# A11 B11 by quarter products, passing weight sets by VectorE or from DRAM, and an order taken from a table

## The chip, the cores and the metric

One core of a Trainium2 chip. TensorE multiplies, VectorE (DVE in the profile) and ScalarE (ACT) work on results and inputs, GpSimd (POOL) can help with sums, SyncE (SP) issues nearly all DMAs. The metric is the device time of one launch in microseconds (us).

## The reference

```python
def reference(x, w):          # x: 8 x 2048 x 2048, w: 2048 x 2048, float32
    cs = np.cumsum(x, axis=1)
    diff = cs - np.concatenate([zeros, cs[:, :-1, :]], axis=1)
    return np.matmul(diff, w)
```

The difference of a running sum is x itself, so what must be computed is x (16384 x 2048, in 128 tiles of 128 rows) times w (2048 x 2048).

## The kernel before

**Outer products.** Tiles 0 to 3 are multiplied plainly in bf16 while w arrives; this also finds w's largest element. From tile 4 on everything is float16, each row of x divided by its scale and w by its largest element. Four tiles make a group: g, h = g + 2, and g + 1, h + 1. A group is called here by the number of its first tile: 4, 8, 12, ... 124, 31 groups. Tile g is the upper half and g + 1 the lower half of a 2 x 2 block matrix, K and N are halved too, and the Strassen-Winograd scheme makes the product with seven products instead of eight: A11 B11, A12 B21, S1 T1, S2 T2, S3 T3, S4 B22 and A22 T4. S1 to S4 are sums of halves of x, made by VectorE in place (`total`); T1 to T4 are sums of weight blocks, made once. h and h + 1 do the same with the same weights. An outer product of one tile is 16 matmuls of 128 x 128 by 128 x 512, so 32 for the pair g, h.

**Inner products by quarters.** Some of the seven are taken once more by the same scheme: g is now the upper, h the lower half, and K and N are halved again. Seven quarter products of 4 matmuls, 28 instead of 32, take its place. Each needs its own weight set of four 128 x 512 blocks: t11, t12, t21, t22 as they stand, Q1 to Q4 as sums (class `Inner`). Group 4 (`group_plain`) has no inner products, groups 8 and 12 have three (A12 B21, S4 B22, A22 T4), and from group 16 on S1 T1 is the fourth (`five` in the code).

**Where results go.** A quarter product ends in one bank of PSUM (eight banks of 128 x 512 float32). An output tile `c` gets its first product by ScalarE (`keep`, L545: bank times the row's unit into SBUF) and each further one by VectorE (`add`, L548: bank times unit plus c). A quarter product that belongs to several outputs is added to each of them.

**Weight sets that pass.** [...] The fourth sets of in_2, in_4 and in_5 go through one small tile, `flow`: in a group VectorE makes one for in_2 (`less`, L501) and one for in_3 (L818), GpSimd makes those of in_5 and in_4 (`pass_fourth`, L505). In groups 8 and 12 some are written to DRAM (`spill`) and fetched back.

**Inputs.** Each tile of x is loaded in two halves (L100), weighed by ScalarE (`weigh`, L112: the sum of absolute values), scaled and narrowed to float16 (`narrow`, L143) and turned by two DMA transposes (`turn`, L156). Five half tiles of float32 (`F`) hold what is on its way: three first halves and two second halves in rotation.

**Order.** Every instruction goes through `after(engine, ...)`, which keeps each engine's instructions in the order in which the code asks for them; each engine takes its queue strictly in order. The order is written out by hand in `group`: products, adds and the steps of S2 T2 and S3 T3 (`go`, 4 matmuls each) are interleaved. Waits on data are put in by the framework.

## Time and profile before

| | us |
|---|---|
| median of 3 runs | 1502.97 (1502.04 to 1503.34) |
| the profiled execution | 1502.15 |
| its span, first to last instruction | 1500.3 |
| PE busy | 1477.7 (98%), 6793 matmuls recorded of 6799 |
| DVE busy | 1329.1 (89%) |
| ACT busy | 914.2 (61%) |
| POOL busy | 329.0 (22%) |
| HBM read, written | 151.52 MB, 136.31 MB |

The busy times come from part 1 of the page. The granted clock of TensorE is full in all slices, and the DMA engines are busy for 80 to 90% of most slices. A line of the groups reads: line of the kernel, engine, operation, tile written <- tiles read, shape, count | busy us, mean ns of one | idle us ahead of it and what ended that idle time.

### The profile page before, as it was taken

The numbers are of one execution on the slowest core, as the hardware profiler recorded it, in microseconds if no ns is written. First come the engines' busy times: TensorE is split into PE (matmuls) and PEld (weight loads), VectorE is DVE, ScalarE is ACT, GpSimd is POOL, SyncE is SP. The second block draws the span as 40 slices with busy tenths as digits, with TensorE's granted clock in tenths as the row PEclk, the third lists the DMA queues.
The fourth block names the chain that finished last, engine by engine and source line by source line (L and its number), as shares of the span: only waits on it lengthen the run. The fifth ranks groups of instructions, "written<-read, shape, count | busy, mean of one in ns | idle before, by whom it ended". The sixth has DMA issues, their size and how long they took to land.

```text
span 1500.3 us, 21209 instructions
## 1 busy us (share of the span) xinstructions
PE 1477.7 (98%) x6793; PEld 660.9 (44%) x6799; DVE 1329.1 (89%) x2419; ACT 914.2 (61%) x1301; POOL 329.0 (22%) x360
## 2 busy tenths in 40 slices
PE   8999999999999999999999999999999999999998
PEld 3444444444444444444444444444444444444443
DVE  7987778889989889998899998889998899898897
ACT  5876565665666655666656666656656656656552
POOL 0100002212221222221222221122222122222122
PEclk9999999999999999999999999999999999999999
DMA  9999989888878898878988887988888988888962
GB/s 358 358 242 273 245 229 238 238 253 237 212 231 218 243 253 224 224 229 220 250 246 213 232 226 227 256 242 214 230 214 240 252 234 220 229 220 241 254 174 106
DMA packets 378913, 354.28 MB, mean 236 GB/s; under 512 B 274929, under 2 KB 275441, under 8 KB 378673
## 3 DMA queue, kind: packets, MB, share of 16 engines
q1 hardware_dynamic: 378240, 351.09, 84.4%
q0 software_dynamic: 560, 1.84, 0.3%
q8 instruction: 53, 0.87, 0.2%
q14 instruction: 60, 0.48, 0.1%
HBM read 151.52 MB, written 136.31 MB: 192 GB/s over the span
## 4 chain that ended last, share of the span: by engine, by line
PE 74%; DVE 13%; issue 4%; DMA 4%; ACT 3%; SPq 0%; DVEq 0%; ACTq 0%
PE b L537 37%; PE b L518 35%; DVE c L548 9%; DVE inner L508 3%; PE b L250 2%; DMA W<-in_w_dram 2%; ACT c L545 2%; DMA F<-in_x_dram 1%; DVE W L501 1%; DMA x<-F 1%; DVE x L508 0%; DMA W<-in_x_dram 0%; DMA out_dram<-c 0%; ACT waste L112 0%; DVE m L129 0%
## 5 line engine op out<-in xcount | busy, mean ns | idle before, releaser
L548 DVE SCALAR_TENSOR_TENSOR c<-b,u,c 128x512 f32<-128x512 f32 x1044 | 734.1, 746 | 125.9 <-PE b L537 76.2
L518 PE MATMUL b<-W,x 128*128 128x512 f16 x3072 | 716.1, 379 | 1.5 <-ACT c L545 0.8
L545 ACT ACTIVATE c<-b,u 128x512 f32<-128x512 f32 x492 | 313.0, 680 | 274.7 <-issue 146.7
L518 PEld LDWEIGHTS <-x 128*128 128x128 f16 x3072 | 300.4, 98 | 364.7 <-DVE x L508 1.7
L143 ACT ACTIVATE F<-F,s 128x1024 f16<-128x1024 f32 x246 | 282.9, 1150 | 162.7 <-DVE s L131 158.7
L537 PE MATMUL b<-W,inner 128*128 128x512 f16 x1392 | 338.3, 379 | 0.0
L112 ACT ACTIVATE waste<-F 128x1024 uint8<-128x1024 f32 x246 | 259.8, 1056 | 119.4 <-DMA F<-in_x_dram 115.4
L537 PEld LDWEIGHTS <-inner 128*128 128x128 f16 x1744 | 168.4, 98 | 215.5 <-DVE c L548 15.4
L132 POOL TENSOR_SCALAR u<-m,uw 128x1 f32<-128x1 f32 x124 | 66.2, 539 | 809.9 <-DVE m L129 802.2
L537 PEld LDWEIGHTS <-x 128*128 128x128 f16 x1560 | 152.1, 98 | 196.0 <-issue 14.4
L537 PE MATMUL b<-W,x 128*128 128x512 f16 x968 | 234.2, 379 | 1.5
L505 POOL TENSOR_TENSOR flow<-W 128x512 f16<-128x512 f16 x140 | 163.6, 1195 | 291.1 <-PE b L537 291.1
L508 DVE TENSOR_TENSOR x<-x,x 128x1024 f16<-128x1024 f16 (+1 forms) x214 | 146.8, 698 | 6.2 <-PE b L518 1.1
L505 POOL TENSOR_TENSOR flow<-W,W 128x512 f16<-128x512 f16 x84 | 94.9, 1160 | 0.0
L537 PE MATMUL b<-flow,x 128*128 128x512 f16 x352 | 90.3, 379 | 2.6 <-DVE c L548 2.6
L508 DVE TENSOR_TENSOR inner<-x,x 128x1024 f16<-128x1024 f16 (+1 forms) x122 | 67.6, 554 | 3.3 <-DMA x<-F 3.3
L537 PE MATMUL b<-inner,x 128*128 128x512 f16 x240 | 61.6, 379 | 0.7 <-DVE x L508 0.7
L250 PE MATMUL b<-wb,xP 128*128 128x512 bf16 x234 | 56.8, 392 | 5.4 <-ACT wb L234 3.8
L537 PE MATMUL b<-inner 128*128 128x512 f16 x240 | 61.6, 379 | 0.5 <-DVE c L548 0.5
L508 DVE TENSOR_TENSOR inner<-x,inner 128x512 f16<-128x512 f16 x60 | 51.7, 862 | 0.0
L112 ACT ACTIVATION_READ_ACCUMULATOR waste<-F 128x1 f32 x246 | 46.7, 190 | 0.0
L508 DVE TENSOR_TENSOR x<-inner,x 128x1024 f16<-128x1024 f16 x62 | 42.4, 683 | 3.2
(58 smaller groups left out, 515.9 us busy)
## 6 DMA issues: line engine op xcount, KB each, us to landing
F<-in_x_dram SPq DMA_DIRECT2D x246, 512.0 KB, 5.0
out_dram<-c SPq DMA_DIRECT2D x492, 256.0 KB, 3.3
W<-in_w_dram SPq DMA_DIRECT2D x32, 512.0 KB, 9.8
W<-in_x_dram SPq DMA_DIRECT2D x16, 256.0 KB, 7.2
x<-F SPq DMA_TRANSPOSE x246, 3.3
spill<-flow SPq DMA_DIRECT2D x3, 512.0 KB, 2.7
out_dram<-o POOLq DMA_DIRECT2D x5, 256.0 KB, 3.9
out_dram<-o SPq DMA_DIRECT2D x5, 256.0 KB, 3.7
```

The source lines that it names most:

```text
L112: lambda: nc.scalar.activation(waste, where[t][i], ABS, scale=1.0 / ROW, accum_out=sums_of[t][:, i : i + 1],),
L132: after("pool", lambda: nc.gpsimd.tensor_scalar(u, m, uw, None, MUL))
L143: lambda: nc.scalar.activation(narrowed(t)[:, ds(i * NH, NH)], where[t][i], COPY, scale=s),
L250: lambda: nc.tensor.matmul(ps[r][n], xP[:, r, ko, :], wb[h, ko][:, ds(n * NB, NB)], start=(ko == 0), stop=(ko == KO - 1),),
L501: after("dve", lambda: nc.vector.tensor_tensor(dst[k], p[k], q[k], SUB))
L505: after("pool", lambda: nc.gpsimd.tensor_tensor(passed[k], i.t21[k], i.Q2[k], SUB))
L508: after("dve", lambda: nc.vector.tensor_tensor(dst.all, p.all, q.all, op))
L518: said = nc.tensor.matmul(to[n], a[k], b[k][:, n, :], start=(first and k == 0), stop=(k == KH - 1), skip_group_check=True,)
L537: said = nc.tensor.matmul(to, a[k], b[k], start=(first and k == 0), stop=(k == 3), skip_group_check=True)
L545: after("act", lambda: nc.scalar.activation(c, p, COPY, scale=u))
L548: after("dve", lambda: nc.vector.scalar_tensor_tensor(c, p, u, c, MUL, ADD))
```

## The change

**A fifth inner product.** A11 B11 is taken by quarters as well (in_1). Group 4 is as before without any, group 8 has two (A12 B21 and S4 B22), and from group 12 on (`more`) there are five: P1 = A11 B11, P2 = A12 B21, P3 = S4 B22, P4 = A22 T4, P5 = S1 T1.

**Sums in the banks.** A new class, `Quarters`, holds one inner product in four banks: h[0], h[1], g[0], g[1]. ScalarE copies product 0 from h[0] to g[0] (`first`), so that product 3 is added to it there by TensorE; products 2, 4 and 6 are added to h[0], and ScalarE copies the state after 2 and after 4 out to a tile in SBUF (`out2`, `out4`). VectorE adds these to h[1], once into g[1] (`middle`) and once in place (`last`). The four banks then hold finished sums, and each output takes one `keep` or one `add` from each. Two tiles (`rooms`) hold s1, s3 and s2, s4 in turn.

**Passing sets.** Seven weight sets pass through `flow` in a steady group. VectorE makes four of them, each in one sum of 128 x 2048 (in3.Q1, in3.Q3, in4.Q1, in1.Q1); three are fetched from DRAM (in1.Q4, in5.t21, in4.Q3), where groups 8 and 12 leave them. GpSimd makes none. All of w stands in one tile, so that one instruction can reach four blocks.

**Buffers.** `F` has four half tiles instead of five, handed out in the order in which they come free. An output tile is 128 x 1024, so it is written by one DMA of 512 KB where there were two of 256 KB.

**Order.** An operation is no longer issued where the code asks for it: `record` notes it under a label, and `emit` issues all of them sorted by a place that a table gives to each label, with a distance of 833 between groups. There are four tables: group 4, group 8, group 12, and one for all later groups.

The diff, cut to this:

```diff
+    def emit(places=None):
+        def when(op):
+            at, label = op[:2]
+            own = places[min(at, 3)]
+            return at * PERIOD + own.get(label, 0)
+
+        for _, _, engine, ask in sorted(ops, key=when) if places else ops:
+            after(engine, ask)
...
-    F = const.tile([P, 5, NH], f32, name="F")
+    F = const.tile([P, 4, NH], f32, name="F")
...
-    def pass_fourth(i):
-        for k in range(4):
-            after("pool", lambda: nc.gpsimd.tensor_tensor(passed[k], i.t21[k], i.Q2[k], SUB))
...
+        def give(self, name):
+            p, q, op = {"Q1": ("t22", "Q2", SUB), "Q4": ("t21", "Q2", SUB), "Q3": ("Q2", "t11", SUB)}[name]
...
+                tensor(f"{self.name}.{name}", flow, self.wide[p], self.wide[q], op)
+            self.b[name] = passed
...
+        def bring(self, name):
+            kept = self.kept
+            record(f"{self.name}.{name}", "sp", lambda: nc.sync.dma_start(flow, kept))
...
+        def middle(self):
+            tensor(f"{self.name}.middle", self.g[1], self.h[1], self.lent, ADD)
+
+        def last(self):
+            tensor(f"{self.name}.last", self.h[1], self.h[1], self.lent, ADD)
+
+        def slot(self, i):
+            h, g, b = self.h, self.g, self.right.b
+            to, left, right, start = (
+                (h[0], "a11", "t11", True),
+                (h[1], "s1", "Q1", True),
+                (h[0], "s2", "Q2", False),
+                (g[0], "a12", "t21", False),
+                (h[0], "s3", "Q3", False),
+                (g[1], "s4", "t22", False),
+                (h[0], "a22", "Q4", False),
+            )[i]
+            quarter(f"{self.name}.{i}", to, getattr(self, left), b[right], start)
+            if i == 0:
+                copy(f"{self.name}.first", g[0], h[0])
+            elif i in (2, 4):
+                copy(f"{self.name}.out{i}", self.lent, h[0])
...
+        P1.slot(0)
+        P1.slot(1)
+        if more:
+            in_1.bring("Q4")
+        ready["tail"]()
+        P1.three()
+        weigh(next_g, [0])
+        P2.slot(0)
+        P2.slot(1)
...
+        P3.middle()
+        P3.slot(3)
+        add("C12g+P3.g", C12g, P3.g, ug, [0])
...
+        if more:
+            in_4.bring("Q3")
```

A stretch of the last table, from P5 into P3 and on to P4, in which a smaller number goes first (`kept` gives the keeps of C22 and C12; `loadN`, `turnN` and `weighN` are those of the tile N places behind the group's first):

```diff
+            'P5.2': 219, 'P5.1': 221, 'P5.out2': 222, 'weigh6.0': 223, 'P5.3': 260,
+            'keep C22g.0': 261, 'keep C12g.0': 262, 'P5.s4': 264, 'P5.s3': 265, 'P5.4': 268,
+            'P5.middle': 320, 'P5.out4': 328, 'P5.5': 329, 'keep C22g.1': 330, 'keep C12g.1': 341,
+            'weigh6.1': 342, ... 'P5.6': 406, 'keep C22h.0': 409, 'P3.0': 414, 'keep C12h.0': 415,
+            'P3.first': 417, 'P3.1': 427, 'narrow6.0': 429, 'narrow6.1': 430, 'P3.2': 434,
+            'P3.out2': 449, 'P3.4': 450, 'keep C22h.1': 451, 'keep C12h.1': 452, 'P3.middle': 469,
+            'P3.out4': 472, ... 'P3.5': 485, 'in4.Q1': 487, 'turn4.1': 489, 'turn6.0': 490,
+            'put0.1': 493, 'P4.0': 497, 'P3.6': 498, 'turn6.1': 505, 'P4.1': 507, 'in4.Q3': 509,
+            'load7.0': 511, ... 'P4.4': 689, 'in1.Q1': 690,
```

## The prediction

> **What bounds the kernel now.** I read the page first, then the chain of waits, then one group cut out of the middle, engine by engine. A group that takes four of the seven outer products by quarters (28 of the 31 do) shows its period in the list of the chain's longest pieces:

> ```profile
> 451.66 6.91 PE b L518 x32
> 497.04 6.91 PE b L518 x32
> ```

> The two starts are 45.38 us apart, and 6.91/32 = 0.2159 us is one matmul of 512 columns. The group has 4 x 28 + 3 x 32 = 208 of them, 44.91 us, so TensorE stands still for 0.47 us in a group. The windows view of just this stretch says how full the others are:

> ```profile
> 820.03:865.41 45.38, 45.26 (x210) 20.25 (x209) 40.97 (x76) 27.87 (x40) 11.18 (x12) 1.00 0.86 235
> ```

> The columns are the length, then PE, PEld, DVE, ACT and POOL busy, the granted clock (1.00), the DMA share and GB/s. TensorE is the bound, VectorE is 90% busy, ScalarE 61%. Where the 0.47 us goes shows in the chain of the same group and in two engines' timelines:

> ```profile
> 842.78 1.36 DVE inner L508
> ...
> 848.52 0.75 DVE c L548
> 849.27 0.04 issue
> 849.32 1.90 PE b L537 x8
> ```
> ```profile
> 841.46 1.40 DVE L508 TENSOR_TENSOR x<-x,x 128x512 f16<-128x512 f16 x1
> 842.77 1.37 DVE L508 TENSOR_TENSOR inner<-x,inner 128x512 f16<-128x512 f16 x1
> ...
> 844.38 12.31 DVE L548 SCALAR_TENSOR_TENSOR c<-b,u,c 128x512 f32<-128x512 f32 x18
> ...
> 864.35 0.42 DVE L508 TENSOR_TENSOR inner<-x,inner 128x512 f16<-128x512 f16 x1
> ```
> ```profile
> 839.18 4.68 POOL L505 TENSOR_TENSOR flow<-W 128x512 f16<-128x512 f16 x4 [4.42 <-PE b L537]
> ```

> While GpSimd makes a passing weight set (839.18 to 843.86), two VectorE sums that take 0.42 us elsewhere take 1.40 and 1.37. The 18 scaled adds behind them run without a gap, and a product that needs their bank starts 0.25 us late. A second stop, 0.21 us at 858.85, is an add between two products of one bank.

> **The change, part by part.** *Fewer matmuls.* A11 B11 by quarters is 28 matmuls for 32. The 28 groups fall from 208 to 204; group 12 has all five sets, so from 212 to 204; group 8 has two, so from 212 to 216. That is 28 x 4 + 8 - 4 = 116 matmuls x 0.2159 = 25.0 us on the path. The floor of a group becomes 204 x 0.2159 = 44.04 us.

> *VectorE, per group, from the table's labels.* Before: 35 adds. After: 20 adds at 12.31/18 = 0.68, 13.7; 10 sums that read a bank and an SBUF tile and write a bank (`middle`, `last`); 20 half-width sums at 0.38 (0.42 alone, 0.34 in a run), 7.6; 8 outer sums at 0.65, 5.2; 4 passing sets of 128x2048; 4 mean-and-reciprocal pairs at 0.37, 1.5. No row shows a sum that writes a bank. Bounds are 0.42 (both inputs SBUF, f16) and 0.75 (the add, which reads a bank); it is nearest the add, so 0.70, 7.0 in all, or 4.2 to 7.5. [...] A 128x2048 sum is 1.22 by the line through 0.42 (512 elements) and 0.69 (1024); four of the narrow ones took 1.42 (row L818, `flow`), so 1.1 to 1.5; 4.9. Sum 39.9 of 44.04: fuller in share than now, but not the bound.

> *ScalarE.* The weighing, narrowing and 16 keeps stay at 27.9. Added are 15 copies from a bank, ten to SBUF and five into another bank:

> ```profile
> L545 ACT ACTIVATE c<-b,u 128x512 f32<-128x512 f32 x492 | 313.0, 680 | 274.7 <-issue 146.7 <-PE b L537 102.0 <-PE b L518 18.6
> L270 ACT COPY o<-b 128x512 f32<-128x512 f32 x9 | 4.7, 601 | 0.0
> ```

> By the copy row 0.52 to 0.60 each, by the keep 0.64 to 0.68: 7.8 to 10.2, I take 0.60, 9.0. ScalarE comes to 36.9, 84% of the group. No row has it write a bank; I take the same price, the bounds hold it.

> *The new links.* Now VectorE adds each quarter product where it lies; after, the products of a set lean on one another through copies. Each of five sets has: product 0, copy, product 2, copy, `middle`, product 5; product 4, copy, `last`, product 6. These ride on TensorE's queue: what waits there holds all products behind it. So I laid the steady table out by hand: 51 steps of four matmuls, 0.864 each, from P1's first at 0, and a result usable 0.2 us after its step (last matmul 379 ns against 216, plus the 0.04 of the chain). The tightest stretch is from P5 to P3. P5.2 ends at 18.1; ScalarE then runs without a pause through out2, a weighing, two keeps, out4, two keeps, a weighing, two keeps, P3's first copy, two narrowings, out2 and the keeps of C22h and C12h, to 30.2. P3.middle writes the bank that these two read, so it runs 30.2 to 30.9, and P3.5 is due at 31.1: 0.15 us to spare. Elsewhere it is 0.35 (P4.0 behind an add), 0.45 (P5.4 behind s3, which waits until P5.1 has read s1), 0.5 (P5.6 behind out4) and more. Nothing is late if durations hold. Some will not quite: I take 0.3 us lost in a group, between 0 and the 0.47 of now.

> *GpSimd.* Its 8 sums a group go: about 1.9 us of VectorE time and the 0.25 us stop with them. What is left there is four one-column products. The passing sets now come through one `flow` tile seven times in a group: four by VectorE (the shortest opening 3.4 us for 1.2 of work), three from DRAM.

> *DMA and SyncE.* Three fetches of 512 KB are added, 1.57 MB on 10.5. 16 writes of 256 KB become 8 of 512. SP has 8 issues fewer there and 3 more, at 0.35 to 0.5 each: a gain hidden anyway. Its queue is in order, and a fetch waits for a product to have read `flow`, with loads and turns behind it. The openings are 7.8, 7.8 and 6.05 us (in4.Q3, after P4.1 and before P4.4). The nearest rows for the landing:

> ```profile
> F<-in_x_dram SPq DMA_DIRECT2D x246, 512.0 KB, 5.0
> ...
> spill<-flow SPq DMA_DIRECT2D x3, 512.0 KB, 2.7
> ...
> flow<-spill SPq DMA_DIRECT2D x1, 512.0 KB, 5.0
> ```

> 5.0 plus 0.4 to issue fits all three, with 0.65 to spare in the tightest. [...] Load buffers fall from five halves to four: each load waits for a narrowing or a turn; by the walk the latest, load7.1 and load5.1, land about when they are due, and ScalarE waits, not TensorE.

> *Set-up.* Group 8 now makes in_1, in_4 and in_5 on VectorE: 44 weight sums x 0.38, three wide ones, 18 adds and the rest come to 46 us beside 216 x 0.2159 = 46.6, some of it put off into group 12. I add 2 us (0 to 5). The end has one more dependent sum and a 512 KB write: 1 us (0 to 2).

> *Sum, against the profiled execution's span:* 1500.3 - 25.0 - 28 x 0.47 (13.2) + 29 x 0.3 (8.7) + 2 + 1 = 1473.8. The execution is 1502.15, 1.85 over its span; the median of the runs is 0.8 above it. So 1473.8 + 2.7 = 1476.5.

> **The rivals.** *A, the gain goes into hand-overs.* The 15 links on ScalarE before P3.middle, and the like in P1 with P2, each cost 0.07 us more than the runs of keeps and weighings show (a bank that TensorE and VectorE also use, a semaphore each). That is 1.1 us lost in a group instead of 0.3: 1476.5 + 29 x 0.8 = 1500, range 1488 to 1506. For it: the smallest slack is 0.15, and ScalarE and VectorE go to 84% and 91%. Against: keeps in a row cost 0.57 apiece at the margin now, under what I charged.

> *B, slower: in4.Q3 lands late.* The page has loads of this size at 5.0, the rows of the tile `F` go up to 7.5, and the DMA share is 0.86 before 15% more bytes in 3% less time, about 0.98 at the same time per byte. Just ahead of this fetch a turn is queued. At 7.5 us P4.4 waits 1.9 us in every group: 1476.5 + 29 x 1.9 = 1532. From 0.9 us late (a landing of 6.5) the kernel is slower than before; I price it 1520, 1503 to 1532. For it too: the fetch has one buffer. Against: a load issued at 848.41, right behind two turns, was there when ScalarE began on it at 852.90, 4.5 us; and the page's first slices move 358 GB/s, while 12.1 MB in 44 us are 275.

> *C, no stops at all:* each slack holds, 1476.5 - 8.7 - 2 = 1465.8. It is the low end of the forecast.

> **How the numbers follow.** Forecast with C 0.68 (1465 to 1488), A 0.16, B 0.16. A measurement of this kernel can tell about 0.2% from no change, 3 us. Faster: 0.68 and half of A, 0.76. Same: a quarter of A and a little of B, 0.05. Slower: the rest, 0.19. The range 1465 to 1503 takes in all but B and A's tail, under 0.2.

> **What would show it.** Starts of the same product 44.1 to 44.6 us apart; 6683 weight loads for 6799; ScalarE some 265 us busier in all, VectorE within 60 us of now, GpSimd under 80; the sum into a bank at 0.65 to 0.75. A would show as TensorE waiting for ACT copies and `middle`, VectorE and ScalarE long in runs; B as TensorE waiting for the DMA into `flow`, fetches landing beyond 6 us. It is wrong if a sum or copy that writes a bank costs over 0.9, if TensorE stops over 1 us in a group at one place, or if the first two groups take 10 us more.

## The result, and the profile after

The changed kernel takes 1460.57 us (median of 4 runs, 1460.01 to 1461.81) against 1502.81: a ratio of 0.972, with a 95% interval of 0.9704 to 0.9737. It is faster, as forecast, by 42.2 us, where the sum said 26.3; 1460.57 lies below the range of 1465 to 1503.

The head of the page after, the starts of a steady run of products in the chain, and the windows view of one group (columns as before):

```profile
span 1458.2 us, 20418 instructions
...
PE 1440.1 (99%) x6677; PEld 652.3 (45%) x6683; DVE 1260.6 (86%) x2292; ACT 1142.9 (78%) x1742; POOL 42.8 (3%) x136
```
```profile
700.19 13.81 PE b L541 x64
744.22 13.81 PE b L541 x64
```
```profile
700.19:744.22 44.03, 44.03 (x206) 19.99 (x204) 38.33 (x71) 35.54 (x56) 1.10 (x4) 1.00 0.93 275
```

The period is 44.03 us with 204 weight loads, 0.2158 each, and TensorE is busy for all of it: there is no stop left. VectorE is busy for 38.33 us, ScalarE for 35.54, GpSimd for 1.10. The new operations cost what the sum said; the groups of instructions after:

```profile
L558 ACT COPY chain<-b 128x512 f32<-128x512 f32 x234 | 136.6, 584 | 93.0 <-PE b L541 91.6 <-DVE c L566 1.4
L509 DVE TENSOR_TENSOR b<-b,chain 128x512 f32<-128x512 f32 x234 | 162.1, 693 | 14.9 <-ACT c L555 11.2 <-ACT chain L558 0.6
L509 DVE TENSOR_TENSOR flow<-W 128x2048 f16<-128x2048 f16 x90 | 109.6, 1218 | 0.0
L558 ACT COPY b<-b 128x512 f32<-128x512 f32 x147 | 83.8, 570 | 77.4 <-PE b L541 38.7 <-DVE c L566 37.3
```

A sum that writes a bank takes 0.69 us (I took 0.70), a copy 0.57 to 0.58 (0.60), a passing set in one sum 1.22 (1.22).

A ledger of TensorE's time shows where the 42 us are. The starts of all weight loads are in both traces (6799 and 6683). What a stage takes beyond its count times 0.21585 us is lost (the first row counts from the first weight load, at 1.18 us in both):

| lost by TensorE, us | before | after |
|---|---|---|
| up to the first product of group 4 | 3.5 | 3.7 |
| group 4 | 2.8 | 2.3 |
| groups 8 and 12 before, group 8 after | 4.9 | 0.5 |
| all later groups | 14.7 | 0.0 |
| from the last weight load to the end of the span | 5.8 | 8.4 |

Fewer matmuls bring 25.0, the stages up to the last product 19.6 (26.0 against 6.4 before rounding), and the end costs 2.5: 42.1 between the spans.

### The profile page after: what moved, and what is told of

Read it like the earlier page. It is cut to its first block, busy times and chain, and to the rows that moved or that the text cites. A ratio compares the mean times of both kernels' runs of the same rounds, so it can differ in the third digit from the quotient of the medians.

```text
span 1458.2 us, 20418 instructions
## 1 busy us (share of the span) xinstructions
PE 1440.1 (99%) x6677; PEld 652.3 (45%) x6683; DVE 1260.6 (86%) x2292; ACT 1142.9 (78%) x1742; POOL 42.8 (3%) x136
## 4 chain that ended last, share of the span: by engine, by line
PE 93%; DMA 3%; DVE 1%; ACT 1%; issue 0%; SPq 0%; DVEq 0%; POOL 0%; ACTq 0%
PE b L541 61%; PE b L522 31%; DMA W<-in_w_dram 3%; PE b L286 1%; DVE W L392 1%; DMA out_dram<-c 1%; ACT W L577 0%; DVE c L566 0%; DMA out_dram<-o 0%; ACT o L304 0%; ACT c L555 0%; DVE b L509 0%; DVE x L509 0%; ACT xP L160 0%; ACT wb L270 0%
## 5 line engine op out<-in xcount | busy, mean ns | idle before, releaser
L522 PE MATMUL b<-W,x 128*128 128x512 f16 x2176 | 524.0, 379 | 0.0
L566 DVE SCALAR_TENSOR_TENSOR c<-b,u,c 128x512 f32<-128x512 f32 x612 | 444.9, 744 | 42.1 <-PE b L541 25.6
L541 PEld LDWEIGHTS <-inner 128*128 128x128 f16 x2700 | 264.0, 98 | 318.8 <-DVE inner L509 0.4
L522 PEld LDWEIGHTS <-x 128*128 128x128 f16 x2176 | 212.9, 98 | 257.1 <-issue 0.7
L541 PE MATMUL b<-W,x 128*128 128x512 f16 x1180 | 293.5, 379 | 0.3 <-ACT b L558 0.3
L541 PEld LDWEIGHTS <-x 128*128 128x128 f16 x1416 | 138.6, 98 | 167.5 <-issue 0.6
L558 ACT COPY chain<-b 128x512 f32<-128x512 f32 x234 | 136.6, 584 | 93.0 <-PE b L541 91.6
L541 PE MATMUL b<-flow,inner 128*128 128x512 f16 x704 | 180.7, 379 | 0.0
L509 DVE TENSOR_TENSOR b<-b,chain 128x512 f32<-128x512 f32 x234 | 162.1, 693 | 14.9 <-ACT c L555 11.2
L558 ACT COPY b<-b 128x512 f32<-128x512 f32 x147 | 83.8, 570 | 77.4 <-PE b L541 38.7
L509 DVE TENSOR_TENSOR flow<-W 128x2048 f16<-128x2048 f16 x90 | 109.6, 1218 | 0.0
L509 DVE TENSOR_TENSOR x<-x,x 128x1024 f16<-128x1024 f16 x124 | 84.8, 686 | 3.1
L509 DVE TENSOR_TENSOR inner<-inner 128x512 f16<-128x512 f16 x116 | 49.3, 425 | 30.0 <-PE b L541 27.9
## 6 DMA issues: line engine op xcount, KB each, us to landing
out_dram<-c SPq DMA_DIRECT2D x248, 512.0 KB, 5.4
F<-in_x_dram SPq DMA_DIRECT2D x246, 512.0 KB, 5.8
flow<-kept SPq DMA_DIRECT2D x87, 512.0 KB, 4.3
W<-in_w_dram SPq DMA_DIRECT2D x32, 512.0 KB, 9.6
```

Source lines behind the costliest of these rows:

```text
L509: record(label, "dve", lambda: nc.vector.tensor_tensor(dst, p, q, op))
L522: said = nc.tensor.matmul(to[n], a[k], b[k][:, n, :], start=(start and k == 0), stop=(k == KH - 1), skip_group_check=True,)
L541: said = nc.tensor.matmul(to, a[k], b[k], start=(start and k == 0), stop=(k == 3), skip_group_check=True)
L558: record(label, "act", lambda: nc.scalar.copy(to, p))
L566: label, "dve", lambda: nc.vector.scalar_tensor_tensor(c, p, u, c, MUL, ADD)
```

## The experiments

All times are medians of several runs, and the ratios are to runs of the kernel before on the same chip (medians 1502.2 to 1503.3).

**e1, A11 B11 whole again.**

```diff
-            if all_seven(g):
+            if False:
                 ready[1] = Quarters("P1", ready["xy"], A11g, A11h, in_1, room(at))
...
```

> The changed kernel with A11 B11 whole in every group (32 matmuls instead of 28; its sums, copies and passing sets are left out), all else and the table as it is. Theory 1 (in the changed kernel TensorE never stands still in a steady group, so time follows the count of matmuls): 29 x 4 = 116 matmuls x 0.2158 = 25.0 us more, 1485.6, and a steady period of 208 x 0.2158 = 44.9 with no gap. Theory 2 (the places of the table fit only the exact set of operations, each shift costs stops): above 1490, with gaps between matmuls.

Measured 1484.50 us, 0.9879 (0.9866 to 0.9893). (In group 12 two steps of P1 changed places, which alters a part of that group's sums, not the number or kind of its operations.) Theory 1 holds: 23.9 us more than the changed kernel for 116 matmuls, and the later groups lose 0.2 us in all. So of the 42 us about 24 hang on the fifth inner product, and 18 come without it.

**e2, the kernel before without GpSimd's sums.**

```diff
     def pass_fourth(i):
-        for k in range(4):
-            after("pool", lambda: nc.gpsimd.tensor_tensor(passed[k], i.t21[k], i.Q2[k], SUB))
+        return
```

> The kernel before without its 8 GpSimd sums in a group (the fourth sets of in_4 and in_5 are left out; stale ones are multiplied). Theory 1 (the 0.25 us stop of each group comes from VectorE sums that wait for GpSimd's reads): VectorE sums at 0.42 instead of 1.40 and 1.37, the stop gone in 28 groups, 7 us less, 1496; the 0.21 us stop stays. Theory 2 (the stop is the chain of adds on one bank): 1502 to 1503, both stops stay.

Measured 1495.64, 0.995 (0.9938 to 0.9963): 7.6 us less. The two groups of sums that took 713 and 862 ns on average before, and the chain's starts:

```profile
L507 DVE TENSOR_TENSOR x<-x,x 128x512 f16<-128x512 f16 x90 | 35.3, 420 | 4.4 <-PE b L517 1.1 <-DVE x L507 0.5
L507 DVE TENSOR_TENSOR inner<-x,inner 128x512 f16<-128x512 f16 x60 | 25.1, 418 | 0.1
```
```profile
541.38 6.91 PE b L517 x32
586.49 6.91 PE b L517 x32
```

The sums are back at 0.42 and the period is 45.11 instead of 45.38: the 0.25 us stop was GpSimd's, the other 0.2 stays. Theory 1 holds. The waits of the kernel before list none of TensorE for GpSimd, so it was not a wait for the sets themselves that went. The 0.98 us added to a sum (1.40 against 0.42) is under the 1.17 (4.68/4) of one GpSimd sum; what holds the VectorE sum up while GpSimd works, no run shows.

**e3, the changed kernel without its table**, and **e10, the same without the fetches.**

```diff
-    emit(places)
+    emit()
```
```diff
         def bring(self, name):
-            kept = self.kept
-            record(f"{self.name}.{name}", "sp", lambda: nc.sync.dma_start(flow, kept))
             self.b[name] = passed
```

(In e10 the first of these is made too; `kept` is still set and not used.)

> The changed kernel issued in the order in which the code asks for its operations, without the table. Theory 1 (the zero stops rest on the places: the steady walk had slacks of 0.15 to 0.5 us): TensorE waits at several links of each group, at least 1 us in 29 groups, 1490 or more. Theory 2 (fewer matmuls and sums in the banks carry the gain by themselves, any sensible order hides the links): 1460 to 1466.

> The changed kernel in the order of the code, as in e3, and without the three fetches of weight sets from DRAM (in1.Q4, in5.t21 and in4.Q3 are left out, what lies in flow is multiplied instead). e3 took 1828. Theory 1 (without its table the change loses most by fetches that stand late in SyncE's queue; the trace of e3 has TensorE wait 341 us for them): 1500 to 1580. Theory 2 (the links between products, copies and sums cost as much, the fetches only come last): above 1650.

Measured 1828.05 (ratio 1.2145, 1.2118 to 1.2173) and 1660.90 (1.1053, 1.1034 to 1.1071). Without the table the kernel takes 367 us more than with it, nearly nine times what the change brings. The waits of e3 and then of e10 (who waited for whom: us in total, times, longest):

```profile
PE b L541 <- DMA flow<-kept: 223.5, 59, 5.4
...
PEld L541 <- DMA flow<-kept: 117.4, 28, 5.0
```
```profile
PEld L541 <- issue: 190.6, 330, 3.9
ACT c L558 <- DMA out_dram<-c: 142.6, 27, 6.9
...
PE b L541 <- ACT c L558: 88.0, 34, 3.6
```

In code order a fetch stands behind writes and turns in SyncE's queue and TensorE waits for it; without the fetches 167 us go. But 200 us of loss stay: e10 lies on theory 2's side, with copies that wait for an output tile still being written and products that wait for copies. Its largest row, 190.6 us of TensorE, names nothing that was waited for, so the waits do not account for all of it. Both parts need the order. Not all of the loss is waiting, either: the mean granted clock is 0.93 in e3 and 0.96 in e10 against 0.998. From 76 us on, TensorE is busy for 203 and 89 us at half the clock (the changed kernel for none), and half of that is lost: some 100 of the 367 us and 45 of the 200 (see the last section).

**e4, one passing set by GpSimd.**

```diff
+            if self.name == "in3" and name == "Q1":
...
+                record("in3.Q1", "pool", some)      # four gpsimd.tensor_tensor
```

> The changed kernel with one of the four passing sets, in3.Q1, made by GpSimd in four sums of 128x512 instead of by VectorE in one of 128x2048. Its opening is long enough: P5.3 has read flow at 20.05 us of the group, P3.1 needs the set at 25.90, and four GpSimd sums took 4.68 in the kernel before. Theory 1 (GpSimd's reads hold up VectorE's sums of two SBUF tiles): S2h, S4h, P4.s1, P3.s1 and P3.s2 lie in this opening, each up to 1 us longer, less 1.2 saved; VectorE is some 3 us late at P3.s1, TensorE stops about 2 us in each group, 1500 to 1530. Theory 2 (who makes the set does not matter while it is there in time): 1460 to 1463.

Measured 1465.56, 0.9757 (0.9742 to 0.9771): 5.0 us more, between the theories. The hold-up is there:

```profile
L509 DVE TENSOR_TENSOR inner<-x 128x512 f16<-128x512 f16 x118 | 71.2, 604 | 0.0
L509 DVE TENSOR_TENSOR x<-inner,x 128x1024 f16<-128x1024 f16 x62 | 53.7, 867 | 1.1
```

These were 0.42 and 0.69 in the changed kernel. Yet the groups from 16 on lose 0.9 us in all: VectorE has room for it. The profiled execution lost the rest in groups 4, 8 and 12, 5.0 us more than the changed kernel's, of which the 1.8 in group 4 lie ahead of the first moved set: there the granted clock fell after a pause (0.52 from 92.5 to 96.0 us; last section), as in e1, which loses 4.0 us in group 4 and moves no set. So that part does not come from GpSimd, and for the rest it is not shown. Theory 1's price was wrong, and "none by GpSimd" is not what a steady group lives on.

**e5 and e6, ScalarE's tightest stretch lengthened.**

```diff
         P3.slot(2)
+        if more:
+            for i in range(1):                    # e6: range(2)
+                copy(f"more{i}", spent, B11[0][:, 0, :])
...
```

> The changed kernel with one more ScalarE copy (128x512 float16 within SBUF, to a tile that nobody reads) between P3.out2 and keep C22h.1 in the 29 later groups, about 0.57 us. Theory 1 (the stretch from P5.out2 to P3.middle is the tightest, and the trace shows 0.35 us to spare between the end of P3.middle and P3.5): 0.2 us stop in a group, 6 us more, 1465 to 1468. Theory 2 (ScalarE's idle 16% takes it up): 1460 to 1462.

> As before with two more copies, 1.15 us. Theory 1: 0.8 us stop in each of 29 groups, 23 us more, 1480 to 1487. Theory 2: 1460 to 1463.

Measured 1461.07 and 1478.63 (0.9841, 0.9827 to 0.9856). One copy costs nothing; two cost 18 us, and by the weight loads TensorE loses 0.61 us in each of the later groups. So the stretch has a knee near 0.55 us, not at the 0.35 I expected: the two copies move P3.middle by 1.17 us in its group, and 1.17 - 0.61 = 0.56. In the timeline of the changed kernel the keeps, and behind them P3.middle, which waits for ScalarE:

```profile
728.90 0.56 ACT L558 COPY chain<-b 128x512 f32<-128x512 f32 x1
729.37 1.27 ACT L555 ACTIVATE c<-b,u 128x512 f32<-128x512 f32 x2
```
```profile
730.67 0.70 DVE L509 TENSOR_TENSOR b<-b,chain 128x512 f32<-128x512 f32 x1 [0.39 <-ACT c L555]
```

P3.middle ends at 731.37, and P3.5's first weights are loaded from 731.76: 0.39 us. But its matmul starts 0.21 us after its weight load does (1446.64 and 1446.85 at another product), and in e6 it is the matmul that waits for the bank: 0.39 + 0.21, less the 0.05 from the end of the sum to the matmul there, is 0.55. The other two traces bear this out. In e5 the sum ends at 732.17 and the matmul starts on time at 732.26. In e6 the weight load still comes on time, at 738.72, but the sum ends at 739.50 and the matmul starts at 739.55. The two links there read

```profile
DVE b L510 <- ACT c L556: 44.6, 28, 1.9
...
PE b L542 <- DVE b L510: 13.7, 28, 0.8
```

**e7 and e11, the fetch of in4.Q3 made later.**

```diff
+                for i in range(3 if self.name == "in4" else 1):
                     said = nc.sync.dma_start(flow, kept)
...
```
```diff
         if more:
+            for i in range(2):
+                extra_write(i)                    # 512 KB of W to a scratch in DRAM
             in_4.bring("Q3")
...
```

> The changed kernel with the fetch of in4.Q3 issued three times, one behind the other, into the same tile with the same data: 1 MB more in each of 29 groups. In the trace the single fetch lands 3.7 us after its issue, 2.0 before P4.4 (0.65 at the least). Theory 1 (transfers of one queue land one behind the other, 1.3 to 2 us per 512 KB): P4.4 waits 0.6 to 2 us, 1478 to 1520. Theory 2 (they overlap, the DMA engines have room): 1460 to 1463.

> The changed kernel with two extra writes of 512 KB (a weight block that never changes, to DRAM that nobody reads) issued in each of 29 groups just ahead of the fetch of in4.Q3; nothing waits for them and they wait for nothing. 1.05 MB more on 12.1 in 44 us. Theory 1 (the DMA engines are nearly full, the page shows 93% of their time taken): in4.Q3 lands over 2.0 us later and the loads late too, TensorE stops 0.6 us or more in a group, 1478 to 1500. Theory 2 (e7 lost its 7 us by holding SyncE's queue, not by bytes; the engines still have room): 1460 to 1464.

Measured 1668.25 (1.1106, 1.1089 to 1.1122) and 1531.58 (1.0186, 1.0166 to 1.0206). e7 costs far more than either theory said, and its SyncE timeline and waits tell why:

```profile
822.78 6.96 SPq L630 DMA_DIRECT2D flow<-kept  x3
```
```profile
SPq L630 <- DMA flow<-kept: 174.2, 59, 4.2
```
```profile
PE b L541 <- DMA flow<-kept: 136.4, 30, 5.8
```

Each further fetch into the same tile waited on SyncE for the one ahead, so the queue was held for 7 us, with loads and writes behind it; TensorE waited 4.5 us for it in a group, and ScalarE for loads. The 136.4 us are two thirds of the 208 lost; nearly all the rest comes from the halved clock behind these pauses (TensorE busy for 138 us at half the clock, so 69 lost). That is a hold-up of a queue, not a test of bytes. e11 is that test, since its writes wait for nothing: in4.Q3 lands 6.7 us after its issue instead of 3.7, and TensorE waits for it in 27 groups:

```profile
PE b L541 <- DMA flow<-kept: 53.8, 27, 2.9
```

Here theory 1 holds, beyond its price. The two writes hold SyncE for 1.0 us, so the fetch is issued 1.05 us behind the last product that reads `flow` instead of 0.03, and it lands 3.0 us later from there: 4.0 in all, past the 2.0 that it had to spare, which leaves the 2.0 us (53.8/27) that TensorE waits. 71 us are lost; in the profiled execution, 79 us above the changed kernel's, 53.8 are this wait and some 15 more the halved clock behind it (TensorE busy for 31 us at half the clock). The changed kernel stands 2 us from a bound by the DMA queue. Whether 1 MB spread over the group would cost as much was not run.

**e8 and e9, the first groups of the kernel before.**

```diff
-        keep_flow(0)
...
-                keep_flow(1)
```
```diff
         put(C11h[1], h, 1)
         weigh(next_h)
         load(next_k, 1)
+        if g == PLAIN + 4:
+            sums_h()                              # S1h, S3h, S2h; they stood further up
         total(S4g, A12g, S2g, SUB)
...
```

> The kernel before without the two writes of flow to DRAM that nothing reads back (keep_flow(0) in group 4, keep_flow(1) in group 12). Theory 1 (the 7.7 us that TensorE loses in groups 4 to 12 come from SyncE's queue, which stands up to 7.0 us at such a write with turns and loads behind it): 3 to 6 us less, 1497 to 1500. Theory 2 (they come from VectorE's weight sums or from the transfers themselves): 1502 to 1503.

> The kernel before with S1h, S3h and S2h of group 8 asked for after the add of product 6's forerunner (C11h[1]) instead of ahead of it; nothing else moved. TensorE loses 4.4 us in group 8 there. Theory 1 (VectorE, in order, stands at S1h until the turn of tile 11 has landed at 142.0 us, and the adds behind it come late): about 2 us of the 4.4 come back, 1501, and the stop of 1.9 us at 145.1 is gone from the trace. Theory 2 (TensorE would wait for the same transfer or for weight sums a little later): the loss of group 8 stays 4 to 5 us, 1503.

Measured 1501.75 (0.9988, 0.9979 to 0.9997) and 1501.72 (0.999, 0.998 to 0.9999): 1.5 and 1.6 us less. In group 8, where the loss is, neither does what theory 1 said: TensorE loses 4.4 us there before, 4.4 in e8 and 4.1 in e9. In e9 the stop at 145.1 us is gone and others of 1.0, 0.5 and 0.4 us stand behind it. The loss looks like a late input chain that moves from one wait to the next; what starts it stays open.

**e12, a shorter end.**

```diff
+    tail_of["C22h+Y.0"], tail_of["C22h+Y.1"] = 735.5, 735.6
+    tail_of["C21h+P4.h.1"], tail_of["C21h+P4.h.0"] = -26.5, -26
...
+                for n in (1, 0):                  # last tile: two writes of 256 KB
```

> The changed kernel with another end of the last group alone: C22h+Y ahead of C21g+P4.g.1, C21h+P4.h.1 ahead of C21h+P4.h.0 on VectorE, and the last 512 KB written as two of 256 KB. The end, from the last weight load to the last instruction, is 8.4 us in the changed kernel and 5.8 in the one before. Theory 1 (2.5 us of the end are VectorE's six operations in a row after P4.5 and the one large write): 1 to 2 us less, 1458.5 to 1459.5, the end at 6.5 to 7.5. Theory 2 (the end is bound by the write's landing alone): within 0.5 us of 1460.6.

Measured 1462.91 (0.9739, 0.9725 to 0.9754), 2.3 us more than the changed kernel, which was measured at another time; the end takes 9.8 us in its trace. Theory 1 is wrong: VectorE's six operations run from 1449.96 to 1454.08 (1449.64 to 1453.62 in the changed kernel), and the writes behind them end it. No version beat the changed kernel.

## Why the prediction was right and wrong

*Matmuls, right.* 25.0 us were predicted; the weight loads show 116 fewer at 0.2158, and e1 gives 23.9 back.

*The new operations, right.* All three prices without a row lay within 0.03 us of what was taken, and VectorE and ScalarE ended at 38.3 and 35.5 us where the sum had 39.9 and 36.9. Both stay under the 44.03 of TensorE. Three of the signs it named were missed by a little: the period lies under 44.1 to 44.6, ScalarE rose by 229 us where it said 265, and VectorE fell by 68 where it said within 60.

*Stops left in a group, wrong: the main miss.* The step "Some will not quite: I take 0.3 us lost in a group", 8.7 us in all, measured 0.0. The walk itself held: P3.middle was laid at 30.2 to 30.9 us and ran from 29.99 to 30.69 in the trace (730.67 less 700.68, the first weight load of P1 in that group). But it counted the spare time to the product's step, that is to its weight load; what waited for the bank in e6 was the matmul, which starts 0.21 us later, so a spare time counted to it is 0.2 longer than written. e5 and e6 find the knee at 0.55 where the walk had 0.15. A loss was then added that no link of the walk showed.

*Stops taken away, too small.* 28 x 0.47 = 13.2 were subtracted; the 28 groups lost 14.7, as the first of them, group 16, lost 1.95 by itself. e2 shows 7.6 us of the removed stops to be GpSimd's; that e4 keeps nearly all of the steady gain with a GpSimd set shows that in the new order there is room for one. What took away the other 0.2 us of a group no run takes alone; e1, with whole A11 B11, has none of it left.

*Set-up, wrong sign.* "I add 2 us (0 to 5)" counted VectorE's work in group 8 against TensorE's and left out what the kernel before lost in groups 4 to 12: 7.7 us, of which 2.8 are left. The term should have been -4.9, 6.9 us away. What removed the loss of group 8 stays open; it is gone in e1 too (0.4 us). The windows of before that would have shown it were not cut by group there.

*The end, too small.* 1 us was taken, 2.5 measured.

The four terms make up the miss: 8.7 + 1.5 + 6.9 - 1.5 = 15.6 us between 26.5 predicted and 42.1 measured by the spans.

*The rivals.* A did not come: no hand-over cost more than charged. B did not come either, yet its mechanism is the real edge: in4.Q3 landed in 3.7 us where 5.0 was taken, 2.0 us of landing were to spare, and e11 used them up. (The DMA share that it feared, 0.98, is 1.02 by its own figures, 0.86 x 1.15 / 0.97; the group measured 0.93.) C, "no stops at all", was the true case; 1465.8 was its price only because set-up still stood in it with 0 and not -4.9. The chance that the forecast shared with C was right, its low end was not: a bound that kept a loss of before inside.

## What to carry to other kernels

Cut the profile before into stages by the starts of the bound engine's instructions and write down what each stage loses; a change to the order can win back all of it, so that ledger, and not only the steady stage, gives the low end. A spare time is to be counted to the instruction that waits for the shared buffer, not to the one that is issued ahead of it (here the matmul, 0.21 us behind its weight load). Where a hand-made schedule is laid out link by link and each holds, add no loss that no link shows; ask instead how far the nearest queue is from its edge, and try that edge.

## What the runs showed of the hardware beyond that

```profile
87.31:90.73 3.42, 2.43 (x12) 0.88 (x9) 2.97 (x5) 3.42 (x5) 0.00 (x0) 1.00 0.99 315
90.73:94.14 3.41, 2.37 (x11) 1.10 (x12) 3.34 (x7) 3.38 (x5) 0.00 (x0) 1.00 0.79 305
```
```profile
89.71:93.13 3.42, 1.43 (x8) 0.61 (x7) 3.35 (x7) 3.42 (x5) 0.00 (x0) 1.00 0.98 371
93.13:96.54 3.41, 3.41 (x10) 1.22 (x8) 3.02 (x7) 1.95 (x4) 0.00 (x0) 0.50 0.22 88
```
```profile
639.84:643.25 3.41, 1.51 (x7) 0.49 (x5) 1.89 (x3) 2.22 (x4) 0.00 (x0) 1.00 1.19 204
643.25:646.67 3.42, 1.75 (x9) 0.81 (x10) 1.72 (x4) 0.67 (x3) 0.28 (x1) 1.00 1.18 263
646.67:650.08 3.41, 3.41 (x17) 1.56 (x16) 2.58 (x5) 3.31 (x4) 0.00 (x0) 1.00 1.05 364
```

The pause of e1 lies in one step, and the next step runs at half the clock: eight matmuls instead of sixteen, some 1.7 us lost, and then the clock is back. The longer pause of e3 is shared by two steps and costs no clock. From 78 us on, the 14 traces have 5740 steps at full clock: with up to 1.95 us of idle time in a step the next one never ran at half clock (5623 steps), from 1.97 us on it always did (117 steps). (Idle time is counted by the ends of matmuls that the trace models.) The 1.6 us by which e1 loses more than the changed kernel in group 4, and most of the 1.8 of e4, come from this; the kernel before and the changed kernel have no such step between 16 us and their last 10 us, so their 42 us owe nothing to it.
